# Moving pool sums behind the first gates, and the decay matrix E into one exponential placed behind weight splits

## The chip, the cores and the metric

The kernel runs on one core of a Trainium2 chip. The metric is device time in microseconds (us) of one execution, and lower is better. The engines are named as the profile names them: PE is TensorE (matmuls; PEld is its weight load), DVE is VectorE, ACT is ScalarE, POOL is GpSimd and SP is SyncE, which only issues DMAs here.

## The reference

One layer of a streaming encoder, for 256 prompt frames and 8 x 16 sample frames together, so T = 384 columns:

```python
u = RMSNorm(x); P = u @ w_in            # columns: pool | z | xBC | dt | gates
# branch A: sliding means with windows 2, 4, 8, 16, minus the frame itself, per-group linear map
win = s[..., i] - s[..., i - w]; d = win / min(w, pos + 1) - p
# branch B: causal conv (4 taps) + SiLU on x, B, C, then the scan by chunks
decay = exp(where(causal, cum[t] - cum[s], -inf))
y = (C.B * decay) @ (x * dt) + (C @ h) * exp(cum)
# merge, then MLP
m = sigmoid(g_A) * (A @ w_pool_proj) + sigmoid(g_B) * (B @ w_ssd_proj); x += RMSNorm(m @ w_out)
x += RMSNorm(relu(RMSNorm(x) @ w_up)^2 @ w_down)
```

All of it is float32, with 64 heads in 8 groups. The sums over time of the decays, `cum`, only fall, so `cum[t] - cum[s]` is at most zero where it counts.

## The kernel before

**Weights and matmuls.** A float32 product is made from parts: a weight tile W of 128x1024 is split into a high part (`wh`, by ScalarE, line 70) and a low part (`wl`, by VectorE, line 71), and each product is three matmuls: wh with the high part of the activations (line 98), wh with their low part (line 99), wl with the high part (line 100). A unit is one output tile of 128 channels over 384 columns; it has two halves of eight weight blocks (24 matmuls) each. Weight tiles come by DMA on SP's queue. The raw tiles, the high parts and the low parts have three buffers each, so a split can run at most three halves ahead of the matmuls, and the buffer for it comes free when the half three earlier is done.

**Order.** Each engine works through its own queue in order. A scheduler sets that order when the program is built, from dependencies and expected durations; `issue_after` adds an ordering. `later()` puts what is in it behind the newest splits (the instructions kept in `cut`, one on ScalarE and one on VectorE) in the order of the program. In the SSD stage, the list `queue` holds the weight halves in order, and `take` has up to three splits issued ahead.

**The pool stage.** `pool_tile` handles one of 16 tiles: it multiplies the projection by the norm into one of two buffers (`pbuf`), places the saved state beside it, sends the new state out by a POOL DMA, and then makes the sliding sums (`win`, line 393), the difference `d` (lines 396 to 409) and its split `dh`, `dl` (lines 412 and 413). The first five projections are made ahead. After the sixth tile (group 1, second tile) come four gate units, `gate_a`, and then the linear map of pool group 0, `pool_map`. The map of a later group reads `dh` and `dl` of its four tiles.

**The SSD stage.** Eight groups g, each with ten units: B, C and four x units (each with a 4-tap convolution: one scaled copy on ScalarE, three `cacc` instructions on VectorE, line 582, and a SiLU, line 586), then four z units (SiLU, line 905). The four head pairs of a group are handled in two "pairs", each with four heads. Between units TensorE does lumps of small matmuls, in a fixed order (`lump`): transposes, C.B, y and state updates. `t_Y` reads the decay matrix E.

E of one pair is a tile of 128 x 4 x 512, made by `eside(S, q)`, two heads for each q, from `cum` of the pair's heads (`cbc`, spread over all partitions by a DMA on SP's queue) and the per-row values in `tok`. Before, each head has one direct exponential of 128 columns (line 747) and three Relu of 128 columns (line 749); then two exponentials per q over the Relu results (lines 757 and 758), and one product with the masked C.B on VectorE (line 759). E has one buffer. `eside` of pair 1 is called during the B and C units of the following group, that of pair 0 after the last x unit and after the first z unit. ScalarE loads a table when it changes between SiLU and exponential. After the second z unit, `finish` normalises the preceding group's result; its squares are summed by POOL (line 815), and its high part is `nh_g` (line 186), its low part `nl_g` (line 187).

Of the kernel before, what the change touches and what calls it, by code (L numbers as in the profile page):

```python
# [9 lines left out]
AF = mybir.ActivationFunctionType  # L10
ALU = mybir.AluOpType
# [3 lines left out]
P = 128  # L15
T = 384
TP = 256
NB = 8
# [6 lines left out]
WINDOWS = (2, 4, 8, 16)  # L25
# [8 lines left out]
def build(ctx, tc, io):  # L34
    nc = tc.nc
    v, s, te, gp, sy = nc.vector, nc.scalar, nc.tensor, nc.gpsimd, nc.sync
# [19 lines left out]
    def behind(ins):  # L56
        return nullcontext() if ins is None else tc.issue_after(ins.ins)
# [16 lines left out]
    @contextmanager  # L74
    def later():
        with behind(cut[0]), behind(cut[1]):
            yield
# [10 lines left out]
    def even_odd(a):  # L88
        return a.rearrange("p (n a) -> p a n", a=2)

    def halves(a):
        return a.rearrange("p (a n) -> p a n", a=2)
# [33 lines left out]
    def proj(units, rhs, name, hook=None):  # L126
        o = bank[0](f"pj_{name}")[:, :T]
        for q, src in enumerate(units):
            half(o, q, take(src, f"{name}_{q}"), rhs)
            if hook:  # L130
                hook()
        return o
# [75 lines left out]
    def in_units(i):  # L208
        return [win[i - 5, 0], win[i - 5, 1]]
# [143 lines left out]
    tok = small.tile([P, 11, NH], F32, name="tok")  # L353
    decb = small.tile([P, NH, NB], F32, name="decb")
    with tc.tile_pool(name="phc", bufs=1, reuse_waits="tile") as pc, tc.tile_pool(name="phc2", bufs=2, reuse_waits="tile") as pc2:
# [3 lines left out]
        for i in range(2):  # L359
            b = pc.tile([P, 640], F32, name=f"pbuf{i}")[:, :519]  # L360
# [5 lines left out]
        dd = [[None] * 4 for _ in range(4)]  # L366

        def pool_tile(gi, k4):
            w = WINDOWS[gi]
            k = gi * 4 + k4  # L370
            ps = early[k] if k < 5 else proj(in_units(1 + k), xg, f"p{k}")
            bf = bufs[k % 2]
            pv = bf[:, 15:271]
            sv = bf[:, 271:].rearrange("p (b t) -> p b t", b=NB)
            po = even_odd(ps)
            v.tensor_tensor(pv[:, :192], po[:, 0], rstd[:, :192], ALU.mult)
            v.tensor_tensor(pv[:, 192:], po[:, 1, :64], rstd[:, 192:TP], ALU.mult)
            v.tensor_tensor(
                sv[:, :, 15:],
                po[:, 1, 64:].rearrange("p (b t) -> p b t", b=NB),  # L380
                rstd[:, TP:].rearrange("p (b t) -> p b t", b=NB),
                ALU.mult,
            )
            s.copy(sv[:, :, :15], pst[:, k])
            stg = pc2.tile([P, 9, 15], F32, tag="stg", name=f"pstg{k}")
            s.copy(stg[:, 0, :], bf[:, 256:271])
            s.copy(stg[:, 1:, :], sv[:, :, 16:])
            gp.dma_start(io["new_pool"][k], stg)
            cur, sh = bf, 1
            while sh < w:  # L390
                nx = pc2.tile([P, 519], F32, tag="win", name=f"win{k}_{sh}")
                lo = 2 * sh - 1
                v.tensor_tensor(nx[:, lo:], cur[:, lo:], cur[:, lo - sh : 519 - sh], ALU.add)
                cur, sh = nx, sh * 2
            d = pc2.tile([P, T], F32, tag="d", name=f"d{k}")
            v.scalar_tensor_tensor(
                out=d[:, :TP], in0=cur[:, 15:271], scalar=1.0 / w, in1=pv, op0=ALU.mult, op1=ALU.subtract
            )
            v.scalar_tensor_tensor(
                out=d[:, TP:].rearrange("p (b t) -> p b t", b=NB),  # L400
                in0=cur[:, 271:].rearrange("p (b t) -> p b t", b=NB)[:, :, 15:],
                scalar=1.0 / w,
                in1=sv[:, :, 15:],
                op0=ALU.mult,
                op1=ALU.subtract,
            )
            rc = cst[:, C_RC + gi * 16 : C_RC + gi * 16 + 16]
            v.tensor_tensor(d[:, :16], cur[:, 15:31], rc, ALU.mult)
            v.tensor_tensor(d[:, :16], d[:, :16], pv[:, :16], ALU.subtract)
            h = pc.tile([P, T], F32R, tag=f"dh{k4}", name=f"dh{k}", bufs=1)  # L410
            l = pc.tile([P, T], F32R, tag=f"dl{k4}", name=f"dl{k}", bufs=1)
            s.activation(h, d, AF.Copy)
            v.tensor_tensor(l, d, h.bitcast(F32), ALU.subtract)
            dd[gi][k4] = (h, l)

        def pool_map(gi, after=None):
            for hf in range(2):
                h, l = wload(io["pool_w"][gi, hf], f"pw{gi}_{hf}")
                for n2 in range(2):
                    n = gi * 4 + hf * 2 + n2  # L420
                    o = sstile(f"pw{n}")[:, :T]
                    with behind(after):
                        for k in range(4):
                            c = slice((n2 * 4 + k) * P, (n2 * 4 + k + 1) * P)
                            mm3w(o, h[:, c], l[:, c], dd[gi][k][0], dd[gi][k][1], k == 0, k == 3)
                    ah, al = (halves(a) for a in A[n])
                    sc = vec[:, V_PSC + n : V_PSC + n + 1]
                    s.activation(ah, even_odd(o), AF.Copy, scale=sc)
                    v.scalar_tensor_tensor(
                        out=al, in0=even_odd(o), scalar=sc, in1=ah.bitcast(F32), op0=ALU.mult, op1=ALU.subtract  # L430
                    )

        def gate_a(i):
            ps = proj([io["w_ga"][i, q] for q in range(2)], xg, f"ga{i}")
            sg = pc2.tile([P, T], F32, tag="sg", name=f"sg{i}", bufs=5)
            v.tensor_tensor(halves(sg), even_odd(ps), halves(rstd), ALU.mult)
            s.activation(sg, sg, AF.Sigmoid)
            return sg
# [6 lines left out]
        def dt_phase(pb):  # L445
            ps = mmtile("pj_dt")[:, :T]
            for q in range(2):
                w = wpool.tile([P, 1024], F32, tag="w", name=f"w_dt{q}")
# [12 lines left out]
            raw, ab, e, t1, t2, q = (n64(x) for x in ("raw", "ab", "e", "t1", "t2", "q"))  # L461
# [16 lines left out]
            dt, cum = n64("dt"), n64("cum")  # L478
# [5 lines left out]
            nb = n64("nb")  # L484
            tot = pb.tile([NH, 1], F32, name="tot")
            v.tensor_tensor(tot, cum[:, 127:128], cum[:, 255:256], ALU.add)
            v.tensor_scalar(nb[:, :P], cum[:, :P], cum[:, 127:128], -1.0, ALU.subtract, ALU.mult)
            v.tensor_scalar(we[:, :P], cum[:, :P], tot, -1.0, ALU.subtract, ALU.mult)
            v.tensor_scalar(we[:, P:TP], cum[:, P:TP], cum[:, 255:256], -1.0, ALU.subtract, ALU.mult)
            cs = cum[:, TP:].rearrange("h (b t) -> h b t", b=NB)  # L490
# [15 lines left out]
        def dt_turn(srcs):  # L506
            for r in range(2):
# [5 lines left out]
                    tok[:, r * 8 : r * 8 + len(part), :].rearrange("p a h -> p (a h)"), o[:, : len(part) * NH]  # L513
                )

        for gi in range(4):
            for k4 in range(4):
                pool_tile(gi, k4)
                if gi and k4 == (gi == 1):
                    if gi == 1:  # L520
                        bank[0] = sstile
                        sg = [gate_a(i) for i in range(4)]
                        bank[0] = mmtile
                    pool_map(gi - 1, last[0])
        srcs = dt_phase(pc)
        pool_map(3)
        for nb in range(4):
            if nb:
                sg = [gate_a(nb * 4 + i) for i in range(4)]
# [13 lines left out]
    with tc.tile_pool(name="phd", bufs=2, reuse_waits="tile") as pd, tc.tile_pool(  # L543
# [5 lines left out]
        for i in range(3):  # L549
            b = pd1.tile([P, 24, 19], F32, name=f"cbuf{i}")  # L550
# [191 lines left out]
        def eside(S, q):  # L742
            if q == 0:
                S.E = pd.tile([P, 4, 512], F32, tag="E", name=f"E{S.nm}", bufs=1)
            for hh in (q * 2, q * 2 + 1):
                ch = S.cbcs[q][:, hh % 2]
                s.activation(S.E[:, hh, P:TP], ch[:, P:TP], AF.Exp, bias=tok[:, 9, S.h0 + hh : S.h0 + hh + 1])
                for b, e0 in enumerate((0, TP, T)):
                    s.activation(
                        S.E[:, hh, e0 : e0 + P],  # L750
                        ch[:, b * P : b * P + P],
                        AF.Relu,
                        bias=tok[:, b, S.h0 + hh : S.h0 + hh + 1],
                        scale=-1.0,
                    )
            Eq = S.E[:, q * 2 : q * 2 + 2]
            s.activation(Eq[:, :, :P], Eq[:, :, :P], AF.Exp, scale=-1.0)
            s.activation(Eq[:, :, TP:], Eq[:, :, TP:], AF.Exp, scale=-1.0)
            v.tensor_tensor(Eq, Eq, S.D.cbm.unsqueeze(1).to_broadcast([P, 2, 512]), ALU.mult)

        def dside(S):
            v.tensor_tensor(
# [80 lines left out]
        for g in range(G + 1):  # L843
# [23 lines left out]
            if g:  # L867
                eside(prev.p[1], 0)
# [10 lines left out]
            S = D.p[0]  # L879
# [367 lines left out]
    with tc.tile_pool(name="phg", bufs=1, reuse_waits="tile") as pg, tc.tile_pool(  # L1247
# [9 lines left out]
        for c8 in range(NC):  # L1257
            hh = []
            for f8 in range(8):
                f = c8 * 8 + f8  # L1260
                ps = ups[f] if f < 3 else proj([io["w_up"][f, 0], io["w_up"][f, 1]], xs2, f"up{f}")
                t = pg2.tile([P, T], F32, tag="t", name=f"ht{f}")
# [169 lines left out]
```

## Time and profile before

| | |
|---|---|
| median of 3 runs | 2654.99 us (2654.96 to 2655.07) |
| the profiled execution: its time, its span | 2654.76 us, 2653.0 us |
| busy: PE, DVE, ACT, POOL | 100%, 58%, 44%, 6% of the span |
| granted TensorE clock | 0.999 |
| DMA | 451.48 MB, mean 170 GB/s |

How to read the profile: times are microseconds from the start of the span. A row of the timeline has start, duration, engine, line, operation, output and inputs with shapes and a count, and in brackets the idle time of the engine ahead of it with what ended it. Rows of a timeline are merged where equal instructions follow each other ("x3"). A group row has busy time and mean nanoseconds, then idle time ahead. Successive instructions of an engine may overlap by a tenth of a microsecond or so in these rows. Matmuls are pipelined: each takes 0.33 us in the rows, but one starts every 0.16 us.

### The profile page before, as it was taken

How to read it: one execution, taken by the hardware profiler on the slowest of the kernel's cores; microseconds unless marked ns; L12 is line 12 of the kernel's file. 1: busy time of each engine (PE TensorE's matmuls, PEld its weight loads, DVE VectorE, ACT ScalarE, POOL GpSimd, SP SyncE). 2: the span in 40 equal slices, each digit the busy share in tenths (PEclk: the TensorE clock that was granted, in tenths of full speed). 3: DMA queues.
4: the chain of work that ended last, by engine and by line, in shares of the span. 5: the costliest groups of instructions: out<-in, count | busy, mean ns of one | idle time of the engine just before them, and what ended most of it. 6: DMA issues, size and time to landing. Idle time of an engine off the chain costs nothing.

```text
span 2653.0 us, 40481 instructions
## 1 busy us (share of the span) xinstructions
PE 2640.3 (100%) x16181; PEld 2539.1 (96%) x16181; DVE 1528.4 (58%) x2152; ACT 1171.7 (44%) x1828; POOL 150.5 (6%) x198
## 2 busy tenths in 40 slices
PE   9999999999999999999999999999999999999998
PEld 9999999999999999999999989999999999989897
DVE  6685334788788888767444436534444444444446
ACT  6443325557565756645333335433333333323233
POOL 0000000011111111020000000000000000000000
PEclk9999999999999999999999999999999999999999
DMA  7444445556666666667554553444444444444443
GB/s 274 146 135 154 147 147 203 194 203 218 207 227 208 211 226 214 224 208 246 177 161 160 186 162 132 143 135 135 135 135 135 135 136 135 136 134 136 136 137 131
DMA packets 147196, 451.48 MB, mean 170 GB/s; under 512 B 18432, under 2 KB 45632, under 8 KB 142016
## 3 DMA queue, kind: packets, MB, share of 16 engines
q1 hardware_dynamic: 134400, 389.90, 44.6%
q0 software_dynamic: 12608, 59.00, 5.9%
q8 instruction: 127, 2.08, 0.3%
q14 instruction: 61, 0.50, 0.1%
HBM read 407.11 MB, written 41.72 MB: 169 GB/s over the span
## 4 chain that ended last, share of the span: by engine, by line
PE 98%; DVE 1%; ACT 1%; issue 0%; DMA 0%; DVEq 0%; ACTq 0%
PE pj_up L98 6%; PE pj_up L99 6%; PE pj_up L100 6%; PE wd L145 6%; PE wd L143 6%; PE wd L144 6%; PE pj_x L98 5%; PE pj_x L100 4%; PE pj_x L99 4%; PE pj_sp L98 3%; PE pj_sp L100 3%; PE pj_z L100 3%; PE pj_z L99 3%; PE pj_sp L99 3%; PE pj_z L98 3%; PE pj_gb L98 2%
## 5 line engine op out<-in xcount | busy, mean ns | idle before, releaser
L98 PE MATMUL pj_up<-x1h,wh_up 128*128 128x384 f32 (+1 forms) x1024 | 333.7, 326 | 0.0
L99 PE MATMUL pj_up<-x1l,wh_up 128*128 128x384 f32 (+1 forms) x1024 | 333.4, 326 | 0.0
L100 PE MATMUL pj_up<-x1h,wl_up 128*128 128x384 f32 (+1 forms) x1024 | 333.4, 326 | 0.0
L71 DVE TENSOR_TENSOR wl_wd<-w_wd,wh_wd 128x1024 fp32r<-128x1024 f32 x126 | 154.4, 1225 | 240.0 <-ACT wh_wd L70 239.8
L143 PE MATMUL wd<-wh_wd,hh 128*128 128x512 f32 x756 | 286.5, 379 | 0.0
L144 PE MATMUL wd<-wl_wd,hh 128*128 128x512 f32 x756 | 286.5, 379 | 0.0
L145 PE MATMUL wd<-wh_wd,hl 128*128 128x512 f32 x756 | 286.5, 379 | 0.0
L70 ACT ACTIVATE wh_wd<-w_wd 128x1024 fp32r<-128x1024 f32 x126 | 133.3, 1058 | 321.6 <-PE wd L145 261.2
L70 ACT ACTIVATE wh_up<-w_up 128x1024 fp32r<-128x1024 f32 x126 | 133.3, 1058 | 292.5 <-PE pj_up L99 231.6
L71 DVE TENSOR_TENSOR wl_up<-w_up,wh_up 128x1024 fp32r<-128x1024 f32 x126 | 154.4, 1225 | 178.8 <-ACT wh_up L70 178.7
L98 PE MATMUL pj_x<-xgh,wh_x 128*128 128x384 f32 x768 | 252.0, 328 | 0.0
L100 PE MATMUL pj_x<-xgh,wl_x 128*128 128x384 f32 x768 | 250.6, 326 | 1.1 <-DVE wl_x L71 1.1
L99 PE MATMUL pj_x<-xgl,wh_x 128*128 128x384 f32 x768 | 250.4, 326 | 0.0
L99 PEld LDWEIGHTS pj_up<-x1l,wh_up 128*128 128x128 f32 x1024 | 193.6, 189 | 0.2
L98 PEld LDWEIGHTS pj_up<-x1h,wh_up 128*128 128x128 f32 x1024 | 193.6, 189 | 0.2
L100 PEld LDWEIGHTS pj_up<-x1h,wl_up 128*128 128x128 f32 x1024 | 193.6, 189 | 0.0
L98 PE MATMUL pj_z<-xgh,wh_z 128*128 128x384 f32 x512 | 166.9, 326 | 0.0
L99 PE MATMUL pj_z<-xgl,wh_z 128*128 128x384 f32 x512 | 166.9, 326 | 0.0
L100 PE MATMUL pj_z<-xgh,wl_z 128*128 128x384 f32 x512 | 166.9, 326 | 0.0
L98 PE MATMUL pj_sp<-abh,wh_sp 128*128 128x384 f32 x512 | 166.9, 326 | 0.0
L99 PE MATMUL pj_sp<-abl,wh_sp 128*128 128x384 f32 x512 | 166.9, 326 | 0.0
L100 PE MATMUL pj_sp<-abh,wl_sp 128*128 128x384 f32 x512 | 166.9, 326 | 0.0
(333 smaller groups left out, 6124.8 us busy)
## 6 DMA issues: line engine op xcount, KB each, us to landing
w_up<-w_up SPq DMA_DIRECT2D x128, 512.0 KB, 3.5
w_wd<-w_down SPq DMA_DIRECT2D x128, 512.0 KB, 3.5
w_x<-w_in SPq DMA_DIRECT2D x96, 512.0 KB, 3.6
w_z<-w_in SPq DMA_DIRECT2D x64, 512.0 KB, 3.6
w_sp<-w_ssd SPq DMA_DIRECT2D x64, 512.0 KB, 3.5
w_ga<-w_ga SPq DMA_DIRECT2D x32, 512.0 KB, 3.5
w_pp<-w_pp SPq DMA_DIRECT2D x32, 512.0 KB, 3.5
hs<-ssm POOLq DMA_DIRECT2D x16, 1024.0 KB, 6.3
```

Of the source, the lines that this page charges most:

```text
L70: cut[0] = s.activation(h, w, AF.Copy)
L71: cut[1] = v.tensor_tensor(l, w, h.bitcast(F32), ALU.subtract)
L98: te.matmul(out, wh, xh, start=first, stop=False, **how)
L99: te.matmul(out, wh, xl, start=False, stop=False, **how)
L100: return te.matmul(out, wl, xh, start=False, stop=last, **how)
L143: te.matmul(out, mh, vh, start=k == 0, stop=False)
L144: te.matmul(out, mh, vl, start=False, stop=False)
L145: last[0] = te.matmul(out, ml, vh, start=False, stop=k == nk - 1)
```

## The change

Three things are changed.

1. `pool_tile` is cut in two. The second part, `pool_rest` (sums, difference, split), of the fifth and the sixth tile is not run at once but after the first and the second `gate_a`, inside `later()`.
2. E is made from four Relu per head, the second block of columns too (for which row 9 of `tok`, `nb`, loses its factor -1), each inside `later()`. One exponential over the whole tile, 128 x 2048, follows in the second call of `eside` (q = 1), with the two products behind it, all inside `later()`.
3. `nb` is one subtraction, without the multiplication in the same instruction.

```diff
         def pool_tile(gi, k4):
-            w = WINDOWS[gi]
             k = gi * 4 + k4
...
             gp.dma_start(io["new_pool"][k], stg)
+
+            def rest():
+                pool_rest(gi, k4, bf)
+
+            return rest
+
+        def pool_rest(gi, k4, bf):
+            w = WINDOWS[gi]
+            k = gi * 4 + k4
+            pv = bf[:, 15:271]
+            sv = bf[:, 271:].rearrange("p (b t) -> p b t", b=NB)
             cur, sh = bf, 1
             while sh < w:
...
-            v.tensor_scalar(nb[:, :P], cum[:, :P], cum[:, 127:128], -1.0, ALU.subtract, ALU.mult)
+            v.tensor_scalar(nb[:, :P], cum[:, :P], cum[:, 127:128], None, ALU.subtract)
...
+        waiting = []
         for gi in range(4):
             for k4 in range(4):
-                pool_tile(gi, k4)
+                rest = pool_tile(gi, k4)
+                if gi == 1 and k4 < 2:
+                    waiting.append(rest)
+                else:
+                    rest()
                 if gi and k4 == (gi == 1):
                     if gi == 1:
                         bank[0] = sstile
-                        sg = [gate_a(i) for i in range(4)]
+                        sg = []
+                        for i in range(4):
+                            sg.append(gate_a(i))
+                            if waiting:
+                                with later():
+                                    waiting.pop(0)()
                         bank[0] = mmtile
...
-                s.activation(S.E[:, hh, P:TP], ch[:, P:TP], AF.Exp, bias=tok[:, 9, S.h0 + hh : S.h0 + hh + 1])
-                for b, e0 in enumerate((0, TP, T)):
-                    s.activation(
-                        S.E[:, hh, e0 : e0 + P],
-                        ch[:, b * P : b * P + P],
-                        AF.Relu,
-                        bias=tok[:, b, S.h0 + hh : S.h0 + hh + 1],
-                        scale=-1.0,
-                    )
-            Eq = S.E[:, q * 2 : q * 2 + 2]
-            s.activation(Eq[:, :, :P], Eq[:, :, :P], AF.Exp, scale=-1.0)
-            s.activation(Eq[:, :, TP:], Eq[:, :, TP:], AF.Exp, scale=-1.0)
-            v.tensor_tensor(Eq, Eq, S.D.cbm.unsqueeze(1).to_broadcast([P, 2, 512]), ALU.mult)
+                for row, t0, e0 in ((0, 0, 0), (9, P, P), (1, P, TP), (2, TP, T)):
+                    with later():
+                        s.activation(
+                            S.E[:, hh, e0 : e0 + P],
+                            ch[:, t0 : t0 + P],
+                            AF.Relu,
+                            bias=tok[:, row, S.h0 + hh : S.h0 + hh + 1],
+                            scale=-1.0,
+                        )
+            if q:
+                with later():
+                    s.activation(S.E, S.E, AF.Exp, scale=-1.0)
+                    for h2 in (slice(0, 2), slice(2, 4)):
+                        Eq = S.E[:, h2]
+                        v.tensor_tensor(Eq, Eq, S.D.cbm.unsqueeze(1).to_broadcast([P, 2, 512]), ALU.mult)
```

## The prediction

> **What bounds the kernel now.** First the page, for the share of each engine:
>
> ```profile
> span 2653.0 us, 40481 instructions
> PE 2640.3 (100%) x16181; PEld 2539.1 (96%) x16181; DVE 1528.4 (58%) x2152; ACT 1171.7 (44%) x1828; POOL 150.5 (6%) x198
> ```
>
> TensorE is busy from end to end, ScalarE 44% and VectorE 58%. No matmul is added, dropped or reshaped, so only TensorE's idle time can change. Second, the waits of TensorE, the ones that this change could touch:
>
> ```profile
> PE pj_ga L100 <- DVE wl_ga L71: 1.5, 1, 1.5
> ...
> PE pj_x L100 <- DVE wl_x L71: 1.1, 2, 0.9
> ```
>
> That is three waits, 2.6 us together, all for the low half (wl) of a weight split: one in the first gates, two in the conv units of group 0. Third, busy time by windows of one group (g) of the SSD stage:
>
> ```profile
> 600.00:690.00 90.00, 90.00 (x666) 87.66 (x665) 74.91 (x108) 57.52 (x112) 12.98 (x13) 1.00 0.64 215
> ```
>
> The columns after the window are its length, PE, PEld, DVE, ACT and POOL busy with counts, the clock (1.00), DMA share and GB/s. In a full group TensorE has no gap, at full clock. So each group can lose, none can win. Time outside the span: the profiled execution took 2654.76 us, 1.76 more than its span and 0.23 less than the median of the runs, 2654.99; I sum on 2654.76 and add 0.23. 0.2% is 5.3 us, about what a measurement of this kernel can tell from no change.
>
> **Part 1, the pool sums behind the gates.** The gate wait on TensorE:
>
> ```profile
> 65.83 0.33 PE L98 MATMUL pj_ga<-xgh,wh_ga 128*128 128x384 f32 x1
> 65.99 0.33 PE L99 MATMUL pj_ga<-xgl,wh_ga 128*128 128x384 f32 x1
> 67.85 0.43 PE L100 MATMUL pj_ga<-xgh,wl_ga 128*128 128x384 f32 x1 [1.53 <-DVE wl_ga L71]
> 68.11 0.33 PE L98 MATMUL pj_ga<-xgh,wh_ga 128*128 128x384 f32 x1
> ```
>
> Matmuls start 0.16 apart; across the wait it is 1.86, and the next step is 0.26. So a wait costs its listed idle time plus 0.17 (overlap lost) and 0.10 (slow restart), 0.27 in all. VectorE around it:
>
> ```profile
> 62.64 0.69 DVE L393 TENSOR_TENSOR win<-pbuf 128x518 f32<-128x518 f32 x1
> 63.25 0.22 DVE L377 TENSOR_TENSOR pbuf<-pj_p,rstd 128x64 f32<-128x64 f32 x1
> ...
> 63.98 0.29 DVE L378 TENSOR_TENSOR pbuf<-pj_p,rstd 128x128 f32<-128x128 f32 x1
> ...
> 65.50 0.55 DVE L436 TENSOR_TENSOR sg<-pj_ga,rstd 128x384 f32<-128x384 f32 x1
> ...
> 66.57 1.22 DVE L71 TENSOR_TENSOR wl_ga<-w_ga,wh_ga 128x1024 fp32r<-128x1024 f32 x1
> ```
>
> In the changed program's built order the instructions up to 62.64 are the same; then stand two evacuations (0.22, 0.29), the gate's product (0.55), one window sum (0.69) and this split (1.22). By whole durations it ends by 62.64 + 2.97 = 65.6, and TensorE's first use would be due at about 65.8 (the built order has dropped the two matmuls hoisted ahead of it). The wait goes; next in line is the split of the third gate, whose matmul is due a half unit, 3.9 us, later. The moved sums, differences and splits of dh and dl are first read by the map of group 1, after the four gates, the map of group 0 and further tiles: no cost. The state copies and the POOL DMA of each tile stay ahead of the gates.
>
> **Part 2, the start of group 0.** E of group 0 leaves the conv units. Table loads there (first and last of five):
>
> ```profile
> 437.22 1.28 ACT L586 ACT_TABLE_LOAD   x1
> ...
> 454.64 1.28 ACT L586 ACT_TABLE_LOAD   x1
> ```
>
> In the built order there is one load in this stretch instead of five, since no exponential alternates with SiLU: 5.1 us of ScalarE less ahead of the late splits, for waits of 1.1. Both go, the first narrowly. Gain of parts 1 and 2: 2.6 + 3 x 0.27 = 3.4 us; bounds 0 (all three stay) and 3.4. The loads of cbc for pair 1 of group 0 move down SP's queue behind weight loads; they are read only after the next pair's transposes, so this costs nothing. The nb instruction keeps its shape: nothing.
>
> **Part 3, E in groups 1 to 7.** Per pair of E nothing shrinks: 16 activations of 128 columns remain, and the exponential over 2048 replaces four. What changes is its place: the `later` fences hold all activations of a half (q) behind the newest split on ScalarE, and the exponential stands in one block with a table load. Two stretches of the built order, the same in groups 1 to 7 instruction for instruction, bring that block directly ahead of a split. I walk them on the clock of the first such group before. An engine's next independent instruction starts about 0.1 before the last one's end (0.05 for short gaps between engines), so I step by duration less 0.1.
>
> *Stretch A, E of the preceding group's pair 1, during the conv units.*
>
> ```profile
> 513.26 0.33 PE L98 MATMUL pj_x<-xgh,wh_x 128*128 128x384 f32 x1
> 517.16 0.33 PE L98 MATMUL pj_x<-xgh,wh_x 128*128 128x384 f32 x1
> ...
> 533.09 0.33 PE L100 MATMUL pj_x<-xgh,wl_x 128*128 128x384 f32 x1
> ```
> ```profile
> 510.16 0.99 ACT L749 ACTIVATE E<-cbc,tok 128x128 f32<-128x128 f32 x3
> ...
> 514.09 0.53 ACT L814 ACTIVATE ysq<-zs 128x384 f32<-128x384 f32 x1
> ...
> 518.05 1.04 ACT L70 ACTIVATE wh_x<-w_x 128x1024 fp32r<-128x1024 f32 x1
> ...
> 524.29 0.62 ACT L586 ACTIVATE xs<-cacc,vec 128x384 f32<-128x384 f32 x1
> ```
> ```profile
> 470.20 1.23 DVE L759 TENSOR_TENSOR E<-E,cbm 128x1024 f32<-128x1024 f32 x1
> 471.33 0.62 DVE L582 SCALAR_TENSOR_TENSOR cacc<-cbuf,vec,cacc 128x384 f32<-128x384 f32 x1
> ...
> 535.03 1.92 DVE L582 SCALAR_TENSOR_TENSOR cacc<-cbuf,vec,cacc 128x384 f32<-128x384 f32 x3
> ```
> ```profile
> L758 ACT ACTIVATE E<-E 128x512 f32<-128x512 f32 x32 | 19.9, 622 | 0.0
> ...
> L757 ACT ACTIVATE E<-E 128x256 f32<-128x256 f32 x32 | 13.1, 409 | 0.1
> ```
>
> A half unit of TensorE lasts 3.9 (513.26 to 517.16) and frees a split buffer; the split into it is used two halves later. The new exponential, from the rows of its two sizes: (622 - 409) / 256 = 0.83 ns an element, 622 + 1536 x 0.83 = 1.90 us. The walk: split at 513.3 (0.95), two squares (0.45 each) to 515.1; eight Relu at 0.30 to 517.5; split, ends 518.56. VectorE: low half 1.13, three taps 1.92, to 521.6. ScalarE waits for them: SiLU 0.53, split 0.95, to 523.1; eight Relu, the last one's end 525.55; table load 1.28, to 526.9; exponential to 528.8. VectorE stands behind it: E product 1.13, tap 0.53, E product 1.13, tap 0.53, to 532.1; only then the low half of the split that TensorE is due to use at 533.09. It takes 1.23, to 533.35, 0.05 for the signal: 0.3 late, with the restart of 0.10 **0.4 us a group**. Bounds: each of about fifteen steps is known to 0.03, so 0 to 0.9.
>
> *Stretch B, E of the same group's pair 0, during the z units.*
>
> ```profile
> 515.09 2.29 DVE L762 TENSOR_TENSOR hs<-hs,decb 128x2048 f32<-128x2048 f32 x1
> ...
> 559.65 1.38 DVE L582 SCALAR_TENSOR_TENSOR cacc<-cbuf,vec,cacc 128x384 f32<-128x384 f32 x1
> ...
> 562.09 0.61 DVE L582 SCALAR_TENSOR_TENSOR cacc<-cbuf,vec,cacc 128x384 f32<-128x384 f32 x1
> ...
> 563.75 3.10 DVE L762 TENSOR_TENSOR hs<-hs,decb 128x2048 f32<-128x2048 f32 x1
> 566.77 0.61 DVE L566 TENSOR_TENSOR cbuf<-pj_x,rstd 128x192 f32<-128x192 f32 x2
> ```
> ```profile
> 572.88 0.55 DVE L187 TENSOR_TENSOR nl_g<-ssum,nh_g 128x384 fp32r<-128x384 f32 x1
> 573.00 0.53 ACT L905 ACTIVATE zs<-zs 128x384 f32<-128x384 f32 x1 [0.65 <-DVE zs L904]
> ```
> ```profile
> 578.77 0.33 PE L100 MATMUL pj_z<-xgh,wl_z 128*128 128x384 f32 x1
> ```
> ```profile
> 514.69 4.70 POOL L815 TENSOR_TENSOR ssum<-ssum,ysq 128x384 f32<-128x384 f32 x1 [0.75 <-ACT ysq L814]
> ...
> 562.70 2.00 POOL L815 TENSOR_TENSOR ssum<-ssum,ysq 128x384 f32<-128x384 f32 x1 [2.08 <-ACT ysq L814]
> ```
>
> Up to the tap at 562.09 VectorE's order is unchanged. The E product that stood after it is gone, so the state product (hs) starts at 562.6 and, taking 3.10 as before, lets the conv evacuation (0.53) end at 566.2. ScalarE: two small copies and the first tap (0.13, 0.12, 0.62) to 567.1. VectorE, after a low half (to 567.3): tap 0.53, nl_g 0.47, two taps to 569.5. ScalarE, which waits for them: SiLU 0.53, eight Relu 2.4, a copy, to 572.65; load 1.28; exponential to 575.85; load 1.28 back to SiLU; SiLU of z 0.43, to 577.6; then the split, ends 578.66. Low half 1.22, 0.05: 579.95, where TensorE is due at 578.77. Late by 1.2, with the restart **1.3 us a group**; the last group's tail has the exponential too, but my walk leaves its split about 1 us early. Both stretches are followed by splits that come in time. Bounds: 0, if the two sums on POOL (below) cost the chain nothing, to 2.1, if VectorE loses 0.8 once more.
>
> Here a rule speaks against the change. ScalarE and VectorE are not saturated (44% and 58%). The Trainium skill, "Perfetto Trace Analysis", section "Optimizing Scalar/DVE Operations", says that where such engines cause bubbles on others, breaking instructions up may let work finish sooner; by it the change, which joins four exponentials to one, would add to the 2.6 us of waits, not remove them. The page gives no size, and the trace of before shows only the split form.
>
> **The sum.** 7 x (0.4 + 1.3) = 11.9 lost, 3.4 won: +8.5. On its own time 2663.3, and with 0.23 more **2663.5 us**. With both stretches at their bounds: 2654.99 - 3.4 = 2651.6 and 2654.99 + 7 x 3.0 - 3.4 = 2672.6.
>
> **The rivals.**
>
> *The freed ScalarE keeps up (2651.6, not slower).* The built order has 38 table loads for 55; 17 x 1.28 = 22 us of ScalarE are saved. If that makes every split early enough, the stretches cost nothing and only the 3.4 is seen. For it: all three old waits end with a late split. Against: two of each full group's six loads go, 2.6 us, but from other places, and the block left in one place (2.4 + 1.28 + 1.9 = 5.6) is longer than a half unit. It decides if my walks are 1.2 too late in B and 0.3 in A. The rule that leads here: the Trainium skill, "ScalarE: Activation LUTs", section "Table sets: the hidden batching unit", tells to batch activations by table set, as the change does; the trace agrees on the price of a load, 1283 ns in the page and 1.28 in the rows. Chance 0.08.
>
> *The sums on POOL fall beside the chain (2654.4, not slower).* In B two instructions of VectorE are long in the trace: a tap of 1.38 for 0.61, a state product of 3.10 for 2.29. Both lie where POOL adds ssum and ysq. These 0.8 each are in my walk. If the additions, which now start somewhat earlier, fall in VectorE's idle time, B shortens by up to 1.6, more than the 1.2, and only A stays: 2654.99 - 3.4 + 7 x 0.4 = 2654.4. Against: VectorE has no idle time from 555 to 569 in the walk. Chance 0.15.
>
> *A long POOL sum holds ScalarE (2669.1, slower still).* nh_g, in ScalarE's queue just ahead of B's block, waits for the second addition. In the walk that addition starts at 562.0. It takes 2.0 in this place before, but another took 4.70; as long as that it would end at 566.7, where nh_g is due at 565.6: 1.1 late, of which other waits absorb some 0.3, so 0.8 more a group, 5.6 us in seven. Chance 0.11.
>
> That the change does not do what it says can be left out for the order, which is built; that the old waits stay in spite of it is the bound 0 of the gain, 3.4 above the forecast and within its range.
>
> **How the numbers follow.** The forecast, both stretches stalling, has 0.65; 0.08 of it is for stalls that sum to less than 8.7, which after the gain is no change. Faster by over 5.3 has no mechanism, since the waits there are hold 3.4: 0.01. Same: 0.08 + 0.08 + 0.15 = 0.31. Slower: 0.57 + 0.11 = 0.68. The range takes in the second rival and most of the third, and leaves out the first and the far end: 2653.0 to 2670.0. The forecast's own range is 2657 to 2669.
>
> **What would show it.** Right: the waits of TensorE list no pj_ga; pj_x for wl_x some seven times by 0.1 to 0.5 (the listed idle time is 0.17 less than the lateness), pj_z for wl_z seven times near 1.0; in the timeline eight Relu, a load and an activation of 128x2048 ahead of each late split. Wrong in the order: no pj_z waits, or waits on another line. Wrong in size: waits on pj_z of some 0.3 (POOL) or near 2. It falls altogether if the time is at or below 2653.

## The result, and the profile after

| | before | after |
|---|---|---|
| median of 7 runs each | 2654.96 us (2654.07 to 2655.23) | 2663.49 us (2662.38 to 2664.29) |
| ratio after / before | | 1.0033, 95% interval 1.0021 to 1.0044 |
| span of the profiled execution | 2653.0 us | 2661.7 us |

The kernel became 8.5 us slower, and 2663.5 had been forecast. The head of the page after:

```profile
span 2661.7 us, 40416 instructions
...
PE 2645.4 (99%) x16181; PEld 2538.9 (95%) x16181; DVE 1524.5 (57%) x2152; ACT 1151.2 (43%) x1763; POOL 131.9 (5%) x198
```

ScalarE has 20 us less to do (1171.7 before) and the kernel is slower all the same. The waits of TensorE after (engine, line, what ended the wait: us in total, times, longest):

```profile
PE pj_z L100 <- DVE wl_z L71: 4.7, 7, 0.7
PE pj_x L100 <- DVE wl_x L71: 1.3, 7, 0.2
```

The gate's wait (pj_ga) is gone, and so are the two waits of 0.9 us and less in the conv units of group 0. In their place stand fourteen new ones, seven of each kind, all for a low half that comes late. The window of one group, beside the one that the prediction shows (PE busy 90.00, 666 matmuls):

```profile
600.00:690.00 90.00, 89.08 (x656) 85.85 (x654) 72.54 (x106) 54.85 (x102) 10.54 (x12) 1.00 0.64 214
```

Ten matmuls fewer start in the same 90 us. At 0.163 us a start that is 1.63 us in a group that had no listed wait before. Below, a loss "by starts" is the distance between the starts of two matmuls, less 0.163, summed over a wait and the slow start after it.

**The gate stage.** VectorE and TensorE, timeline after:

```profile
63.43 0.55 DVE L446 TENSOR_TENSOR sg<-pj_ga,rstd 128x384 f32<-128x384 f32 x1
63.90 0.69 DVE L403 TENSOR_TENSOR win<-pbuf 128x518 f32<-128x518 f32 x1
64.50 1.22 DVE L71 TENSOR_TENSOR wl_ga<-w_ga,wh_ga 128x1024 fp32r<-128x1024 f32 x1
...
65.80 0.33 PE L100 MATMUL pj_ga<-xgh,wl_ga 128*128 128x384 f32 x1
```

One window sum is left ahead of the split. The split ends at 65.72 and TensorE uses it at 65.80 without a wait: there is little to spare, 0.08 us between the two rows.

**Stretch A**, the first time it comes (ScalarE, VectorE, TensorE; timeline after):

```profile
522.29 1.28 ACT L778 ACT_TABLE_LOAD   x1
523.59 1.92 ACT L778 ACTIVATE E<-E 128x2048 f32<-128x2048 f32 x1
...
525.53 1.23 DVE L781 TENSOR_TENSOR E<-E,cbm 128x1024 f32<-128x1024 f32 x1 [3.04 <-ACT E L778]
...
528.87 1.22 DVE L71 TENSOR_TENSOR wl_x<-w_x,wh_x 128x1024 fp32r<-128x1024 f32 x1
...
530.14 0.43 PE L100 MATMUL pj_x<-xgh,wl_x 128*128 128x384 f32 x1 [0.19 <-DVE wl_x L71]
```

VectorE stands idle for 3.04 us in front of the first E product, and the low half is queued behind that. TensorE's start at 530.14 is 0.51 after the one before it (529.63); with the slower start after it the loss is 0.45 us.

**Stretch B**, the first time it comes:

```profile
567.22 2.44 ACT L769 ACTIVATE E<-cbc,tok 128x128 f32<-128x128 f32 x8
...
569.78 1.28 ACT L778 ACT_TABLE_LOAD   x1
571.08 1.92 ACT L778 ACTIVATE E<-E 128x2048 f32<-128x2048 f32 x1
573.01 1.28 ACT L927 ACT_TABLE_LOAD   x1
...
574.74 2.94 ACT L70 ACTIVATE wh_z<-w_z 128x1024 fp32r<-128x1024 f32 x3
...
573.02 2.36 DVE L781 TENSOR_TENSOR E<-E,cbm 128x1024 f32<-128x1024 f32 x2 [4.76 <-ACT E L778]
575.81 2.36 DVE L71 TENSOR_TENSOR wl_z<-w_z,wh_z 128x1024 fp32r<-128x1024 f32 x2 [0.42 <-ACT wh_z L70]
...
575.83 0.43 PE L98 MATMUL pj_z<-xgh,wh_z 128*128 128x384 f32 x1
576.10 0.33 PE L99 MATMUL pj_z<-xgl,wh_z 128*128 128x384 f32 x1
577.09 0.43 PE L100 MATMUL pj_z<-xgh,wl_z 128*128 128x384 f32 x1 [0.67 <-DVE wl_z L71]
```

From the eight Relu on, ScalarE is busy without a break to its first split at 574.74. Both halves of the weight are late: the high one by 0.22 us, the low one by 0.83 more, and each wait has its 0.10 of slow start, 1.26 us in all.

### The profile page after: what moved, and what is told of

Its sections match the earlier page's. It is cut to its first block, busy times and chain, and to the rows that moved or that the text cites. A ratio compares the mean times of both kernels' runs of the same rounds, so it can differ in the third digit from the quotient of the medians.

```text
span 2661.7 us, 40416 instructions
## 1 busy us (share of the span) xinstructions
PE 2645.4 (99%) x16181; PEld 2538.9 (95%) x16181; DVE 1524.5 (57%) x2152; ACT 1151.2 (43%) x1763; POOL 131.9 (5%) x198
## 4 chain that ended last, share of the span: by engine, by line
PE 86%; DVE 5%; ACT 4%; DMA 3%; issue 2%; SPq 0%; DVEq 0%; ACTq 0%; POOLq 0%; POOL 0%
PE pj_up L98 6%; PE pj_up L99 6%; PE pj_up L100 6%; PE wd L145 6%; PE wd L144 6%; PE wd L143 6%; PE pj_sp L100 3%; PE pj_sp L98 3%; PE pj_sp L99 3%; PE pj_x L98 2%; PE pj_x L100 2%; PE pj_x L99 2%; PE pj_z L100 2%; PE pj_z L99 2%; PE pj_z L98 2%
```

## The experiments

Each was timed in five rounds with runs of the kernel before on the same chip (their medians: 2654.5 for the first four, 2654.7 for the others). The theory is that of the prediction: three separate gains at the front, and in each of seven groups two separate stalls, A and B, each because a block stands ahead of a split that TensorE needs next.

### One part of the change at a time

The diff cut in two. `pool_only` has the first part and leaves E and `nb` as before; `e_only` has E and `nb` and leaves the pool tiles as before.

> The kernel before with the first part alone: sliding sums of the fifth and sixth pool tile behind the first two gates, E as before. Theory (three gains and two stalls a group, each by itself): the gate stage's wait, 1.80 us by the starts of its multiplications, goes and nothing else moves: 2655.0 - 1.8 = 2653.2 us, the wait for wl_ga absent, the waits of conv units in group 0 as in before. Rival (the sums only moved the gap to the second gate or to the pool maps): within 0.5 us of before, with a new wait of 1 us or more between 60 and 110 us.

> The kernel before with the second and third part alone: E's Relu steps fenced, one exponential for four heads, the negated sums' sign; the sliding sums as before. Theory: the gate wait of 1.8 us is back and all else as in the changed kernel: 2663.5 + 1.8 = 2665.3 us, seven waits of pj_x for wl_x and seven of pj_z for wl_z. Rival (the two parts disturb each other, the sums being what makes the fenced blocks late): 2655 or less, the fourteen waits gone or smaller than half.

Measured: `pool_only` 2652.8 us (0.9993 of before, interval 0.9984 to 1.0002, so the time alone does not tell it from no change), `e_only` 2664.5 us (1.0038, 1.0025 to 1.0051). The wait of `pool_only` that bears on E:

```profile
PE pj_x L100 <- DVE wl_x L71: 0.9, 1, 0.9
```

And those of `e_only`:

```profile
PE pj_z L100 <- DVE wl_z L71: 4.7, 7, 0.7
PE pj_ga L100 <- DVE wl_ga L71: 1.5, 1, 1.5
PE pj_x L100 <- DVE wl_x L71: 1.2, 7, 0.2
```

The parts add up. With the pool sums alone the gate's wait is absent, the large wait of group 0 stays, and no group stalls. With E alone the gate's wait is back with its 1.5 us, the wait of 0.9 us in group 0 is gone, and all fourteen new ones are there. So E is what costs, and the pool sums have no share in it. `nb` was not tried apart from E.

### Each block moved away from its split

`b_later` calls E's second half and its exponential, for pair 0, one z unit later:

```diff
             pload(D.p[1])
-            eside(S, 1)
             zproj(1)
+            eside(S, 1)
```

`a_late` moves nothing on ScalarE. For pair 1 it takes the two E products out of `eside` and calls them, in `later()`, one conv unit on:

```diff
             D.xs.append(conv(u0 + 2, g * 4, "xs", 6))
             if g:
+                eprod(prev.p[1])
                 dside(prev.p[1])
```

`both_late` has both moves, and `both_late2` is the same kernel once more.

> The changed kernel with the step that makes E of pair 0's second half and its exponential called after the second z unit instead of after the first. The built order then has Silu of zs_0 and wh_z_2_0 ahead of the block, and the exponential behind wh_z_3_0. Theory (block directly ahead of a split whose half unit is next): Stretch B's stall, 7 x 1.26 us by starts, goes, Stretch A stays at 7 x 0.45: 2663.5 - 8.8 = 2654.7 us; in its new place the block has about 1 us to spare before wl_z_3_1. Rival (the work of the block itself is what costs, wherever it stands between two splits): the stall moves to wl_z_3_1 and the time stays within 2 us of 2663.5.

> The changed kernel with only the two E products of pair 1 on VectorE moved one unit on, behind the next split; ScalarE's block (8 Relu, table load, exponential) stays where it is. Theory (Stretch A is VectorE waiting in order for the exponential with the wl split queued behind): A's 7 x 0.45 us go, B stays: 2663.5 - 3.1 = 2660.4 us, no wait of pj_x for wl_x. Rival (ScalarE's own split wh_x behind the block is what is late in A): A's stalls stay, 2663.5.

> The changed kernel with both moves: E's second half and exponential of pair 0 called after the second z unit, and the two E products of pair 1 behind the next split. Theory (two separate stalls, each from a block directly ahead of a split): both go, 2663.5 - 8.8 - 3.1 = 2651.6 us, about 3 us under the kernel before, no wait of pj_x for wl_x and none of pj_z for wl_z. Rival (the stalls only hide later ones): 2654 or more with a wait in another place.

> The kernel with both moves once more, to narrow its comparison with the kernel before: theory 2652.4 us as in the first run, 2.2 under before; rival: no difference from before, within 0.5 us.

| kernel | expected | measured | ratio to before, interval |
|---|---|---|---|
| `b_later` | 2654.7 | 2655.8 | 1.0005 (0.9996 to 1.0014) |
| `a_late` | 2660.4 | 2660.0 | 1.0021 (1.0012 to 1.0030) |
| `both_late` | 2651.6 | 2652.4 | 0.9992 (0.9983 to 1.0001) |
| `both_late2` | 2652.4 | 2653.0 | 0.9994 (0.9985 to 1.0002) |

In `b_later` one kind of wait is left:

```profile
PE pj_x L100 <- DVE wl_x L71: 1.2, 7, 0.2
```

In `a_late` the other:

```profile
PE pj_z L100 <- DVE wl_z L71: 4.7, 7, 0.7
```

With both moves neither kind is listed. The same activations, loads and products run in all of these kernels. Only their place differs, and it decides some 11 us (2663.5 to 2652.4 and 2653.0). `a_late` also shows what A is. ScalarE's block is as it was, and VectorE's low half comes ahead of the E products:

```profile
522.70 1.92 ACT L778 ACTIVATE E<-E 128x2048 f32<-128x2048 f32 x1
...
525.43 1.27 DVE L602 SCALAR_TENSOR_TENSOR cacc<-cbuf,vec,cacc 128x384 f32<-128x384 f32 x2 [3.81 <-ACT cacc L600]
526.62 1.22 DVE L71 TENSOR_TENSOR wl_x<-w_x,wh_x 128x1024 fp32r<-128x1024 f32 x1
...
529.42 1.22 DVE L786 TENSOR_TENSOR E<-E,cbm 128x1024 f32<-128x1024 f32 x1
```

VectorE still stands idle until the block is over, 3.81 us here, for the scaled copy that follows the block on ScalarE, and TensorE does not wait. So the idle time by itself is not the stall. What makes the low half late in A is the two E products that stand between the end of the exponential and the low half in VectorE's queue.

`both_late` is the best version of the whole change that keeps the exponential, about 2 us under before, which these runs do not quite tell from no change. By time it is level with `pool_only` (2652.8). In groups 1 to 7 E by one exponential brings nothing even where it costs nothing, as TensorE had no listed wait there. In group 0 it does remove waits: after the first 20 us, the loss by starts is 3.5 and 3.0 us under before in the two profiles with both moves, and 2.1 in that of `pool_only`. The times do not resolve that difference; those first 20 us alone differ by 1.6 us between the two profiles of the same kernel.

### What in the block counts

`copy_exp` does a plain copy in place of the exponential, so that no table is loaded; E keeps its Relu values. `exp_halves` and `halves_b` break the exponential in two, one per `q`, everywhere or for pair 0 only.

```diff
-                    s.activation(S.E, S.E, AF.Exp, scale=-1.0)     # copy_exp
+                    s.activation(S.E, S.E, AF.Copy, scale=-1.0)
...
-            if q:                                                  # exp_halves
-                with later():
-                    s.activation(S.E, S.E, AF.Exp, scale=-1.0)
+            with later():
+                Eq = S.E[:, q * 2 : q * 2 + 2]
+                s.activation(Eq, Eq, AF.Exp, scale=-1.0)
```

> The changed kernel with the exponential replaced by a plain copy of the same 128x2048 pass, so E keeps the Relu values (the exponential is left out); with it the two table loads around it go, order of everything else as in the changed kernel. Theory: the loads, 1.28 us ahead of the pass and in Stretch B 1.28 behind it, are more than either stall (0.45 and 1.26 us), since the E products start 1.28 us sooner in both: both stalls go, 2663.5 - 12 = 2651.5 us. Rival (the length of the pass and the fences, not the loads): the stalls shrink by less than half, 2657 or more.

> The changed kernel with the exponential broken into two of 128x1024, one after each set of eight Relu steps, each with its own E product and fence; 68 table loads instead of 38. Theory (what stands ahead of the split counts): in A a pass shorter by about 0.9 us and one product of 1.2 less ahead of the split, A's 0.45 us go (-3.1); in B the first half's load, pass and product delay the taps and Silu ahead of the second block by about 1.8 us, the second block is shorter by 0.9 and one product of 1.2, so about 0.3 us of 1.26 go (-2): about 2658 us, between 2655 and 2664. The rule that breaking an instruction up lets work finish sooner gives under 2663.5. Rival (30 more loads of 1.28 us dominate): over 2664.

> The changed kernel with the exponential broken in two for pair 0 only; pair 1 (conv units) keeps one exponential and the built order of the changed kernel. Theory (what the kernel with all exponentials broken lost, it lost in the conv units, where the built order then has a table load and a Silu ahead of wh_x_0; in the z units it gained about 0.25 a group): 2663.5 - 1.8 = 2661.7 us, seven waits of pj_x for wl_x of 0.2 as in the changed kernel, no wait of pj_x for wh_x. Rival (the number of table loads costs in itself): between 2663.5 and 2668.1, about 2665.8 for half of the extra loads.

`copy_exp`: 2650.9 us (0.9986 of before, 0.9977 to 0.9995). ScalarE in Stretch B:

```profile
568.28 1.92 ACT L778 ACTIVATE E<-E 128x2048 f32<-128x2048 f32 x1
...
570.51 1.99 ACT L70 ACTIVATE wh_z<-w_z 128x1024 fp32r<-128x1024 f32 x2
```

The pass is as long as before (1.92) and in the same place, but the split follows 2.2 us after its start instead of 3.7. All fourteen waits are gone, so the two loads of 1.28 us are enough to decide whether B stalls, and the one ahead of the pass decides A. (Of 38 loads in the program 7 are left; ScalarE's other instructions in A and B keep their order.)

`exp_halves`: 2668.1 us (1.0050, 1.0037 to 1.0062), where my theory had 2658. By the time alone the rival, the number of loads, would hold; `halves_b` was made to tell the two apart. The waits of `exp_halves`:

```profile
PE pj_z L100 <- DVE wl_z L71: 5.2, 7, 0.7
PE pj_x L100 <- DVE wl_x L71: 4.7, 7, 0.7
PE pj_x L98 <- ACT wh_x L70: 1.2, 7, 0.2
```

Stretch B shrank as expected, to 1.01 us a group by starts (the high half now comes in time). A grew from 0.45 to 1.37, where I had it gone. ScalarE in A:

```profile
525.65 1.06 ACT L778 ACTIVATE E<-E 128x1024 f32<-128x1024 f32 x1
526.73 1.28 ACT L606 ACT_TABLE_LOAD   x1
528.02 0.61 ACT L606 ACTIVATE xs<-cacc,vec 128x384 f32<-128x384 f32 x1
528.55 1.99 ACT L70 ACTIVATE wh_x<-w_x 128x1024 fp32r<-128x1024 f32 x2
```

With a shorter exponential the scheduler put the load back to SiLU and the SiLU ahead of the high half, which had followed the exponential in the changed kernel. I had taken that order as unchanged. The sum by starts: 7 x (0.92 - 0.25) = 4.7, for the 4.6 us measured. `halves_b` keeps the old order in A, and came to 2661.7 us (1.0026, 1.0016 to 1.0036), the number expected:

```profile
PE pj_z L100 <- DVE wl_z L71: 5.2, 7, 0.8
...
PE pj_x L100 <- DVE wl_x L71: 1.2, 7, 0.2
```

The listed wait in B is longer than in the changed kernel (5.2 for 4.7), but TensorE has waited less for the high half just before it, and by starts B costs 1.06 us a group for 1.25. A and B together gain 1.4 of the 1.8 us; that the time met the expectation to the tenth is luck. So table loads do not cost by their number: the gain in B is there although the program has 54 loads for 38. They cost where they stand ahead of a split.

### GpSimd's additions

`pool_small` adds 8 of 384 columns in each addition of the squares and leaves the rest of that sum out.

```diff
-                    gp.tensor_tensor(D.ssum, D.ssum, qs, ALU.add)
+                    gp.tensor_tensor(D.ssum[:, :8], D.ssum[:, :8], qs[:, :8], ALU.add)
```

> The changed kernel with the GpSimd additions of the squares cut to 8 of 384 columns (the rest of the sum of squares is left out), so that nothing long runs there beside VectorE. Theory (chain: addition on GpSimd, slowed tap 1.36 instead of 0.61 and state product 2.28 instead of about 1.5 on VectorE, last tap, Silu of the conv unit which ScalarE waits 1.46 us for, then the block): Stretch B's block starts up to 1.46 us sooner, its stall of 1.26 us goes or nearly, A stays: about 2655 us. Rival (the additions run beside the chain, VectorE waits 4.8 us for the exponential anyway): 2663 us, both sets of waits as they were.

Measured: 2653.6 us (0.9997, 0.9988 to 1.0006). Of the two kinds only pj_x is left, seven times 0.2. The changed kernel first, around its second addition in Stretch B:

```profile
559.20 1.00 POOL L837 TENSOR_TENSOR ssum<-ssum,ysq 128x384 f32<-128x384 f32 x1 [1.43 <-DMA new_ssm_s<-hs]
...
559.25 1.36 DVE L602 SCALAR_TENSOR_TENSOR cacc<-cbuf,vec,cacc 128x384 f32<-128x384 f32 x1
```

Then `pool_small`, the same tap and the state product behind it:

```profile
558.54 2.46 POOL L837 TENSOR_TENSOR ssum<-ssum,ysq 128x8 f32<-128x8 f32 x1 [1.94 <-ACT ysq L836]
...
558.13 0.61 DVE L602 SCALAR_TENSOR_TENSOR cacc<-cbuf,vec,cacc 128x384 f32<-128x384 f32 x1
558.66 2.28 DVE L784 TENSOR_TENSOR hs<-hs,decb 128x2048 f32<-128x2048 f32 x1
```

Two taps took 0.61 instead of 1.37 and 1.36, so ScalarE could start the SiLU ahead of the block 1.5 us sooner (on the clock of the group), and B, where the low half was 1.2 us late, went. Stretch B is thus a chain that needs both: the block, and the 1.5 us that VectorE loses ahead of it beside GpSimd. My expectation was wrong in one point: the state product takes 2.28 us here too, and 2.29 elsewhere in the kernel before, so in the changed kernel it was not slowed.

### Without the fences

`no_fence` leaves Relu, exponential and products without `later()`.

> The changed kernel without the fences around E's Relu steps, exponential and products; the scheduler places them. In the built order they stand earlier: in groups 1 to 7 all sixteen Relu, the load and the exponential are ahead of wh_x_1 (conv units) and ahead of wh_z_0_1 (first z unit), and the E products ahead of the low halves of these splits. Theory (a block directly ahead of a split costs what it is longer than the time to spare, fence or not): by the rows of the changed kernel the exponential would end near 513.5 and the two products push the low half from 514.1 to 517.0 where it is due at 514.2 (2.8 late), and near 559.2 and 561.6 against 560.0 (1.6 late); the two stalls of 0.45 and 1.26 go: 2663.5 - 12 + 7 x 4.4 = 2682 us, between 2668 and 2695. Rival (the fences themselves cause the stalls): at or under 2655.

Measured: 2655.4 us (1.0002, 0.9993 to 1.0011), far from the 2682 of my theory and close to its rival (at or under 2655). In the conv units the built order was as described. The exponential ended at 516.27, as reckoned (513.5 in the changed kernel; this one is 2.6 later by here). The products took 0.8 longer than reckoned, beside a GpSimd addition. What was wrong is the time at which the low half was due:

```profile
516.30 3.18 DVE L780 TENSOR_TENSOR E<-E,cbm 128x1024 f32<-128x1024 f32 x2 [0.72 <-ACT E L777]
519.40 1.21 DVE L71 TENSOR_TENSOR wl_x<-w_x,wh_x 128x1024 fp32r<-128x1024 f32 x1
...
520.39 0.33 PE L98 MATMUL pj_x<-xgh,wh_x 128*128 128x384 f32 x1
520.55 0.33 PE L99 MATMUL pj_x<-xgl,wh_x 128*128 128x384 f32 x1
520.71 0.39 PE L100 MATMUL pj_x<-xgh,wl_x 128*128 128x384 f32 x1
```

The low half is done at 520.61 and used at 520.71. I had counted it due a half unit (3.9 us) earlier: with three buffers a split may lie two halves ahead of its use, as the prediction had it and the expectation forgot. At that spot the block had room for a whole half more. In the z units the same half unit was left out: the low half is used there at 566.22, 3.9 later than reckoned. What the kernel loses against `both_late` is in group 0, where conv waits are back (1.3 us listed in two waits for the low half, 2.7 by starts with the late high halves), and about 0.2 us a group in the z units. So a block ahead of a split costs only what it exceeds the time to spare, and the fences cost because they hold the block back to a spot with less to spare.

## Why the prediction was right

- **Part 1.** As walked: the split was to end by 65.6 and be due at 65.8, and it ended at 65.72 and was used at 65.80. `pool_only` shows the gain alone: 1.7 us between medians, 1.80 by starts.
- **Part 2.** Both waits of group 0 go. By starts the three waits were worth 3.8 us; the prediction's 2.6 + 3 x 0.27 = 3.4 left out the late high half at the second one (0.28). `e_only` shows that E's new form removes the large one. That it is the missing table loads that do it was not tried apart and stays argued; `no_fence`, with three loads there instead of one, has two waits back.
- **Stretch A.** 0.45 for 0.4, seven times, by the chain that was walked (exponential, E products with taps between them, low half); `a_late` shows that it is the place of the products in VectorE's queue. The exponential took 1.92 where the slope gave 1.90.
- **Stretch B.** 1.26 for 1.3. The walk's end was 579.95 where 578.77 was due. `copy_exp` and `b_later` show the block as the cause. One sign differed: the wait was to be listed near 1.0 and stands at 0.7, because the high half is late as well and part of the loss lies two matmuls ahead. And two terms were sized wrongly against each other: the state product was put at 3.10 and took 2.28, while a second tap was slowed (1.36) that had been counted at 0.61. The second addition on GpSimd came sooner and met the tap instead of the product. That the two offset each other to 0.1 us was luck, as the walk had not foreseen it.
- **The sum.** 7 x 1.71 = 12.0, less 3.8, gives 8.2; measured 8.5. The profiled spans differ by 8.7, and 0.5 of that lies in the start-up, ahead of all the waits treated here. So the agreement of 2663.5 with 2663.49 is closer than the terms are, and in part luck: the gain was 0.4 larger than forecast, and in the profiled executions the start-up took about as much back.
- **"The freed ScalarE keeps up"** did not come: its 20 us less lie elsewhere. It is `copy_exp` that has this rival's time (2651.6 forecast, 2650.9), by taking the loads away from that spot.
- **"The sums on POOL fall beside the chain"** did not come either, but its mechanism is real: with the additions cut, B goes and A stays, 2653.6 against its 2654.4.
- **"A long POOL sum holds ScalarE"**: the second addition ended at 560.2 here, and nh_g waited for nothing.
- **The rule of the Trainium skill**, "Perfetto Trace Analysis", section "Optimizing Scalar/DVE Operations", that breaking instructions up may let work finish sooner, was cited as pointing against the change. The direction came true, but `exp_halves` and `halves_b` show that breaking up is not by itself what helps: 4.6 us more in the one, 1.8 less in the other, as what stood ahead of the splits grew or shrank.

## What to carry to other kernels

When one engine is busy from end to end and others feed it in order, sum nothing over the feeders' busy time: for each instruction that the bound engine waits for, list what the built order puts ahead of it on its own engine, and compare the end of that with the time it is due, counted in buffers. A longer block with less total work can lose against several short ones. The cure here was its place rather than its size: one unit later, or, without the fences, sooner. After any edit look at the built order again, since a shorter instruction can draw a table load to the wrong side of a split.

## What the runs showed of the hardware

**GpSimd beside VectorE.** Cutting GpSimd's additions to one forty-eighth of the columns hardly shortened them in the mean. The group rows of the changed kernel and of `pool_small`:

```profile
L837 POOL TENSOR_TENSOR ssum<-ssum,ysq 128x384 f32<-128x384 f32 x24 | 42.3, 1762 | 26.6 <-ACT ysq L836 23.7 <-DMA new_ssm_s<-hs 2.9
```

```profile
L837 POOL TENSOR_TENSOR ssum<-ssum,ysq 128x8 f32<-128x8 f32 x24 | 38.7, 1613 | 30.2 <-ACT ysq L836 30.2
```

That is 8% less. But the mean misleads, because much of it is waiting, and with 8 columns nearly all. The last addition of each kernel runs while VectorE does nothing, and there the size does count. First the changed kernel, then `pool_small`:

```profile
1185.84 0.99 POOL L837 TENSOR_TENSOR ssum<-ssum,ysq 128x384 f32<-128x384 f32 x1 [0.36 <-ACT ysq L836]
```

```profile
1176.44 0.19 POOL L837 TENSOR_TENSOR ssum<-ssum,ysq 128x8 f32<-128x8 f32 x1 [0.31 <-ACT ysq L836]
```

In Stretch B, in the rows further up, an addition of 8 columns lasts 2.46, until VectorE's state product is over (561.00 against 560.94). In the changed kernel a tap that meets an addition takes 1.36 for 0.61. So one waits for the other; the tap's end does not fit to better than 0.2 us (560.20, where the addition ends, and 0.61 make 560.81, and it ended at 560.61). The Trainium skill, "SBUF — State Buffer", section "SBUF: two separate sides", says that the two engines share a pair of ports, which a VectorE instruction with two inputs in SBUF needs against a GpSimd instruction that reads SBUF; that the one which starts first holds it for its whole instruction, and that the other blocks. The rows agree with a lock. Which of the two had it first they do not settle, since the addition of 8 columns is listed 0.12 us ahead of the product that it waits out.
